# A hybrid diffusion layer: the output projection of the second token block as one seven-product pass

## The chip, the cores and the metric

The kernel runs on one core of one Trainium2 chip. The metric is device time in microseconds (us), the median of three runs. The profile is of one more execution, taken by the hardware profiler. Engines: PE (TensorE), with PEld for its weight loads, DVE (VectorE), ACT (ScalarE), POOL (GpSimd), and SP, whose queue issues every DMA of this kernel.

## The reference

One layer of a diffusion backbone over 2048 latent tokens of width 1024, with 256 context tokens before them. All in fp32:

```
hl  = rms(x) * norm1 * (1 + sc1) + sh1
z, xbc, dt, u, v = split(hl @ w_in)
ssd = rms_per_group((scan(conv(xbc), dt) + skip) * silu(z)) * ssd_norm   # 1024 wide, forward and backward scan
gm  = gelu(u) * (W_s @ rms(gelu(v)) + b_s)                               # 1024 wide, per 128 tokens
x   = x + g1 * (concat(gm, ssd) @ w_out)                                 # w_out 2048 x 1024
hl2 = rms(x) * norm2 * (1 + sc2) + sh2
x   = x + g2 * ((silu(hl2 @ w_gate) * (hl2 @ w_up)) @ w2)                # hidden width 2816
out = rms(x) * final_norm
```

`sc1`, `sh1`, `g1` and the like come from the conditioning vector. The context tokens only give the scans their start states.

## The kernel before

Everything is stored with channels on the 128 partitions and tokens along the row. The 2048 tokens are two blocks of 1024 (block 1 is computed first, since the backward scan starts at its end), each block two groups `j` of 512 tokens. A matmul is 128x128 stationary by 128x512 moving. Each fp32 operand is split into a high and a low part of a reduced type (a ScalarE cast and a VectorE subtract), and each product is three matmuls: high by high, high by low, low by high.

The stages follow each other so. (1) Block 1: `xbc`, then one interleaved run (L937) with the main sequence `proj_v`, `proj_u`, `proj_z` and, beside it, context scan, backward scan, row statistics and `ada_rest`, which loads 16 MB of modulation weights. (2) Block 0: `xbc`. (3) A second interleaved run (L943): the main sequence `proj_z`, `proj_v`, `proj_u`, then `out_half(1, 0)`, `out_half(0, 0)`, `out_half(0, 1)`; beside it the rest of the backward scan and the whole forward scan `ssd_y`. (4) `out_half(1, 1)` alone. (5) `prep_hl(0)`, then `ffn1(0)`, `ffn2(0)` with `prep_hl(1)` beside it, `ffn1(1)`, `ffn2(1)`.

`run` (L871) alternates generators: after each `yield` of the main sequence it advances the other one by a ratio, 1.4 side steps in (1) and `SIDE` = 2.74 in (3). A main step is one output tile, 24 matmuls; `ssd_y` and the backward scan of block 0 have 256 side steps. This program order is a priority: a planner then gives each engine a fixed order of instructions by its own cost estimates and by the buffers that come free, and on the chip each engine and SP take theirs in order.

The output projection works by halves of the inner width: half 0 takes `gm` (kept in `gmscr`), half 1 the scan's output (kept in `sscr` by `y_store`, L781). `out_half` has for each block and half eight output tiles `m` by two groups `j`, each eight inner tiles by three matmuls; it adds to the residual `x2scr` in DRAM. Its moving operands are loaded and split by `load_mix` (L819) into 16 tiles `actt`, its weights are loaded by `unit` (L201) three ahead and split. The sum of squares for the second norm is taken on the way, and its inverse root is stored in `r2scr`.

The feed-forward uses seven products in place of eight (a Strassen scheme) for each 2x2 arrangement of tiles. `prep_hl` (L980) reads `x2scr` and `r2scr`, scales and shifts, forms the four sums that the scheme needs and splits them into 28 tiles `hl`. `ffn1` forms the weight sums on GpSimd as it goes; `ffn2` (L1129) runs product by product: for each product `p` of seven and each inner step `i` it loads two 128x512 tiles (activations from `ascr`, weights from `wscr` or `wall`) into one buffer `w4`, splits it into two buffers `hl4`, and issues four banks by three matmuls. Loads go four steps ahead, splits two. Results accumulate in two sets of four PSUM banks, and after the last step of a product its banks are added to the residual tiles.

The feed-forward's pools (`hlp`, 112 KB per partition; `t2p`, `w4p`, `hlw`, 92 KB) are opened after `mix` and `pjs`, the pools of all that came before, are closed:

```
    for _ in out_half(1, 1, s1):
        pass
    mix.close()
    pjs.close()
    ...
    hl, g = prep_hl(0)
    for _ in g:
        pass
    ffn1(0, hl)
```

## Time and profile before

| | |
|---|---|
| median of 3 runs | 3014.0 us (3011.1 to 3016.5) |
| the profiled execution | 3005.2 us, span 3003.4 us |
| TensorE busy | 94% of the span, 12474 matmuls |
| VectorE, ScalarE, GpSimd busy | 67%, 43%, 21% |
| DMA | 515 MB, mean 172 GB/s |
| granted TensorE clock, mean | 0.967 |

The page cuts the span into 40 slices of 75 us; a digit is the busy share in tenths, PEclk the granted clock in tenths of full speed. By time, (1) reaches to about 590, (2) to 765, (3) to 1551, (4) to 1639, and the feed-forward fills the rest.

### The profile page before, as it was taken

Reading aid. Unit: us, or ns where it says so; the run is one execution under the profiler, and the core shown is the slowest. Engines: PE = TensorE matmul, PEld = TensorE weight load, DVE = VectorE, ACT = ScalarE, POOL = GpSimd, SP = SyncE. Lnnn points to the kernel's source line nnn. Section 1 sums busy time; section 2 is a strip of 40 time slices with the busy share of each in tenths; the row PEclk is TensorE's granted clock in tenths of the full one; section 3 lists DMA queues with packets and bytes.
Section 4 is the critical chain, followed back from the end, with each engine's and each line's share of the span. In section 5 each row is a group of like instructions: output and inputs, shape, how many; then the busy total and the mean of one; then the engine's idle time right before and its main releaser. Section 6 shows DMA issues by size and latency. Waiting matters only on the chain. (4 is left out here: it accounts for less than half of the span.)

```text
span 3003.4 us, 37067 instructions
## 1 busy us (share of the span) xinstructions
PE 2818.3 (94%) x12474; PEld 2252.2 (75%) x12474; DVE 2017.5 (67%) x3412; ACT 1295.1 (43%) x2387; POOL 642.9 (21%) x550
## 2 busy tenths in 40 slices
PE   7999999999999888999898699999999899999997
PEld 3787778878677766777676488888778788888885
DVE  6777966885788878877653755556776644445555
ACT  4444343344355555445442433333554333333443
POOL 3100000110131222223100444445120322221000
PEclk8999999999999999999999699999999999999998
DMA  5322567732755668778644344444766433334764
GB/s 221 97 90 83 190 220 232 257 118 88 240 152 155 209 197 253 239 237 250 197 150 122 106 162 158 158 158 168 257 227 201 150 101 100 102 102 134 235 194 155
DMA packets 289771, 515.45 MB, mean 172 GB/s; under 512 B 28198, under 2 KB 88998, under 8 KB 289580
## 3 DMA queue, kind: packets, MB, share of 16 engines
q1 hardware_dynamic: 289580, 513.08, 53.4%
q8 instruction: 98, 1.61, 0.2%
q14 instruction: 93, 0.76, 0.1%
HBM read 375.60 MB, written 137.38 MB: 171 GB/s over the span
## 5 line engine op out<-in xcount | busy, mean ns | idle before, releaser
L970 DVE TENSOR_TENSOR hl<-w,hl 128x1024 fp32r<-128x1024 f32 x286 | 373.8, 1313 | 313.5 <-ACT hl L969 130.3
L969 ACT CAST hl<-w 128x1024 fp32r<-128x1024 f32 x286 | 299.2, 1051 | 435.9 <-PE mmp L1053 126.7
L228 PE MATMUL mmp<-actt,whi 128*128 128x512 f32 x1120 | 455.5, 407 | 6.2 <-DVE tma L575 6.2
L229 PE MATMUL mmp<-actt,whi 128*128 128x512 f32 x1120 | 445.5, 398 | 0.0
L230 PE MATMUL mmp<-actt,wlo 128*128 128x512 f32 x1120 | 444.2, 397 | 0.0
L1052 PE MATMUL mmp<-hl,hl 128*128 128x512 f32 x704 | 277.7, 394 | 37.1 <-ACT hl L969 32.4
L1053 PE MATMUL mmp<-hl,hl 128*128 128x512 f32 x704 | 276.9, 393 | 2.4 <-DVE hl L970 2.4
L1054 PE MATMUL mmp<-hl,hl 128*128 128x512 f32 x704 | 276.7, 393 | 0.0
L228 PEld LDWEIGHTS mmp<-actt,whi 128*128 128x128 f32 x1120 | 214.7, 192 | 55.4 <-DVE tma L575 7.5
L229 PEld LDWEIGHTS mmp<-actt,whi 128*128 128x128 f32 x1120 | 214.5, 191 | 48.1 <-issue 5.3
L230 PEld LDWEIGHTS mmp<-actt,wlo 128*128 128x128 f32 x1120 | 214.5, 192 | 47.6 <-issue 1.7
L228 PE MATMUL mmp<-whi,actt 128*128 128x512 f32 x512 | 212.1, 414 | 0.0
L1052 PE MATMUL smp<-hl,hl 128*128 128x512 f32 x528 | 209.1, 396 | 1.7 <-ACT hl L969 1.6
L1053 PE MATMUL smp<-hl,hl 128*128 128x512 f32 x528 | 207.5, 393 | 0.0
L1054 PE MATMUL smp<-hl,hl 128*128 128x512 f32 x528 | 207.3, 393 | 0.1
L230 PE MATMUL mmp<-whi,actt 128*128 128x512 f32 x512 | 206.9, 404 | 0.0
L229 PE MATMUL mmp<-wlo,actt 128*128 128x512 f32 x512 | 206.3, 403 | 0.0
L1052 PEld LDWEIGHTS mmp<-hl,hl 128*128 128x128 f32 x704 | 133.7, 190 | 67.6 <-ACT hl L969 34.8
L976 DVE TENSOR_TENSOR t<-smp,t 128x512 f32<-128x512 f32 x88 | 60.5, 687 | 180.5 <-PE smp L1054 105.9
L450 DVE SCALAR_TENSOR_TENSOR tma<-xin,cw,tma 128x512 f32<-128x512 f32 x192 | 144.3, 751 | 21.8 <-ACT tma L448 16.2
L1053 PEld LDWEIGHTS mmp<-hl,hl 128*128 128x128 f32 x704 | 133.9, 190 | 31.2 <-DVE hl L970 3.5
L731 POOL TENSOR_TENSOR tma<-tma 128x512 f32<-128x512 f32 x64 | 88.9, 1389 | 319.8 <-ACT tma L730 223.0
(256 smaller groups left out, 5816.5 us busy)
## 6 DMA issues: line engine op xcount, KB each, us to landing
w<-in_wall_dram SPq DMA_DIRECT2D x110, 512.0 KB, 4.0
ws<-in_wall_dram SPq DMA_DIRECT2D x104, 512.0 KB, 4.2
ascr<-t SPq DMA_DIRECT2D x154, 256.0 KB, 4.1
w<-ascr SPq DMA_DIRECT2D x154, 256.0 KB, 2.7
tma<-fscr SPq DMA_DIRECT2D x128, 256.0 KB, 5.5
w<-wscr SPq DMA_DIRECT2D x88, 256.0 KB, 3.5
w<-in_wall_dram SPq DMA_DIRECT2D x66, 256.0 KB, 4.0
rec<-tma SPq DMA_DIRECT2D x64, 256.0 KB, 2.6
```

Source lines behind the costliest of these rows:

```text
L228: PE.matmul(ps, lhsT=lh, rhs=rh, start=(i == 0), stop=False)
L229: PE.matmul(ps, lhsT=lh, rhs=rl, start=False, stop=False)
L230: PE.matmul(ps, lhsT=ll, rhs=rh, start=False, stop=(i == n - 1))
L450: V.scalar_tensor_tensor(out=acc[:, :n], in0=raw[:, j:j + n], scalar=cw[:, ch, j:j + 1], in1=acc[:, :n], op0=ALU.mult, op1=ALU.add)
L731: G.tensor_tensor(out=A, in0=A, in1=fb, op=ALU.mult)
L969: S.copy(hi, x)
L970: eng.tensor_tensor(out=lo, in0=x, in1=hi.bitcast(F32), op=ALU.subtract)
L976: eng.tensor_tensor(out=o, in0=a, in1=b, op=ALU.add)
L1052: PE.matmul(ps, lhsT=hi[:, ms_], rhs=t[:, 0, :], start=first and k == 0, stop=False, skip_group_check=not first)
L1053: PE.matmul(ps, lhsT=hi[:, ms_], rhs=t[:, 1, :], start=False, stop=False, skip_group_check=not first)
L1054: PE.matmul(ps, lhsT=lo[:, ms_], rhs=t[:, 0, :], start=False, stop=k == 3, skip_group_check=not first)
```

## The change

The output projection of block 0 stays as it was. That of block 1 becomes one pass of seven products over both halves, by the routine of `ffn2`, which is made general (`product_major`) and gives a `yield` after each step. The pass, `out_pm(1)`, has eight inner steps in place of the feed-forward's eleven; four take `gm`, four the scan's output.

Its operands are built earlier. `proj_u(1)` forms the sums of `gm` tiles (two subtracts on GpSimd, two on VectorE for each pair of heads) and stores seven tiles in `ogm` instead of four. `y_store` stores the chunks 8 to 11 unchanged in `osd`; for each of the chunks 12 to 15 it reads two of those back, does four subtracts on VectorE and stores five tiles. `wo_sums`, at the end of the side sequence of (1), loads the projection's weights (given once more as `wok`), scales them on ScalarE, forms four sums on GpSimd for each of eight groups and stores seven tiles per group in `owt`; the ratio there becomes 1.6.

The pass is the end of the main sequence of (3): after `out_half(0, 1)` the pool `pjs` is closed and the streaming buffers are opened in its place, on the right side of the memory. The side sequence goes on after `ssd_y` with `prep_hl(0)`, six side steps for each of its four parts, once `mix` is closed. Two product steps count as one main step, and the pass does not go beyond its eighth step before `ssd_y` is done. `SIDE` becomes 3.1.

```diff
-SIDE = 2.74
+SIDE = 3.1
...
+    wp = pjs.enter_context(tc.tile_pool(name="wp", bufs=NWP, side="right"))
+    ws = pjs.enter_context(tc.tile_pool(name="ws", bufs=2, side="right"))
+    ap_ = pjs.enter_context(tc.tile_pool(name="act", bufs=16, side="right"))
+    xi = pjs.enter_context(tc.tile_pool(name="xin", bufs=NX, side="right"))
...
+    sp = mix.enter_context(tc.tile_pool(name="sml", bufs=8))
...
+    ogm = [tc.dram_tile([7, P, TB], F32, name=f"ogm{i}") for i in range(4)]
+    osd = [tc.dram_tile([4, P, TB], F32, name=f"osd{i}") for i in range(7)]
+    owt = [tc.dram_tile([7, P, TB], F32, name=f"owt{i}") for i in range(8)]
...
-    order += (list(range(U_O, U_O + 8)) * 2 + list(range(U_O + 8, U_O + 16)) * 2)
+    order += list(range(U_O, U_O + 16))
...
+            bs = {}
...
-                    t = gelu2(ps, tmp)
+                    t = gelu2(ps, xin if blk else tmp)
                     V.tensor_tensor(out=t[:, :TB], in0=t[:, :TB], in1=m[:, :TB], op=ALU.mult)
-                    DMA.dma_start(gmscr[h0 + i][:, ts_], t[:, :TB])
+                    if blk == 0:
+                        DMA.dma_start(gmscr[h0 + i][:, ts_], t[:, :TB])
+                    else:
+                        bs[i, j] = t[:, :TB]
+                        if len(bs) == 4:
+                            b11, b12, b21, b22 = bs[0, 0], bs[0, 1], bs[1, 0], bs[1, 1]
+                            t1, tt, t4 = tmp()[:, :TB], tmp()[:, :TB], tmp()[:, :TB]
+                            sub(t1, b12, b11, G)
+                            sub(tt, b22, t1, V)
+                            sub(b12, b22, b12, G)
+                            sub(t4, b21, tt, V)
+                            for q, x in ((1, b11), (2, b21), (6, tt), (5, t1), (7, b12), (3, b22), (4, t4)):
+                                DMA.dma_start(ogm[h0 // 2][AQ[q]], x)
...
     def y_store(ys, c):
+        bs = []
         for g in range(2):
             ps = smp()
             for i in range(4):
                 PE.transpose(out=ps[:, i * P:(i + 1) * P], in_=ys[g][:, i * P:(i + 1) * P], identity=ident)
             t = tma()[:, :TB]
             S.copy(t, ps)
-            DMA.dma_start(sscr[c // 4][g * TB:(g + 1) * TB, (c % 4) * P:(c % 4 + 1) * P].rearrange("(i p) t -> p i t", p=P),
-                          t.rearrange("p (i t) -> p i t", t=P))
+            if c < 8:
+                DMA.dma_start(sscr[c // 4][g * TB:(g + 1) * TB, (c % 4) * P:(c % 4 + 1) * P].rearrange("(i p) t -> p i t", p=P),
+                              t.rearrange("p (i t) -> p i t", t=P))
+            bs.append(t)
             yield
+        if c < 8:
+            return
+
+        def osl(q):
+            return osd[AQ[q]][:, :, (c % 4) * P:(c % 4 + 1) * P].rearrange("i p t -> p i t")
+
+        def v4(t):
+            return t.rearrange("p (i t) -> p i t", t=P)
+
+        if c < 12:
+            DMA.dma_start(osl(1), v4(bs[0]))
+            DMA.dma_start(osl(2), v4(bs[1]))
+            return
+        b12, b22 = bs
+        b11, b21, tt = tma()[:, :TB], tma()[:, :TB], tma()[:, :TB]
+        DMA.dma_start(v4(b11), osl(1))
+        DMA.dma_start(v4(b21), osl(2))
+        sub(b11, b12, b11, V)
+        sub(tt, b22, b11, V)
+        sub(b12, b22, b12, V)
+        sub(b21, b21, tt, V)
+        for q, x in ((6, tt), (5, b11), (7, b12), (3, b22), (4, b21)):
+            DMA.dma_start(osl(q), v4(x))
...
+    def wo_sums():
+        for i in range(8):
+            k1, k2 = (2 * i, 2 * i + 1) if i < 4 else (4 + i, 8 + i)
+            q = []
+            for k in (k1, k2):
+                for h in range(2):
+                    t = tma()[:, :TB]
+                    DMA.dma_start(t, wok[k][:, h * TB:(h + 1) * TB])
+                    S.activation(t, t, AF.Copy, scale=0.5 if i < 4 else vec[:, V_SN + k - 8:V_SN + k - 7])
+                    q.append(t)
+            a0, a1, b0, b1 = q
+            s1, s2, s4 = tma()[:, :TB], tma()[:, :TB], tma()[:, :TB]
+            add(s1, a1, b1, G)
+            sub(s2, s1, a0, G)
+            sub(s4, b0, s2, G)
+            sub(a1, a0, a1, G)
+            for p, x in ((1, a0), (2, b0), (6, s2), (5, s1), (7, a1), (3, s4), (4, b1)):
+                DMA.dma_start(owt[i][AQ[p]], x)
...
-        (chain(ssd_ctx(rp, hp), ssd_bwd(rp, hp, range(15, 7, -1)), stats_x(0, tma), stats_x(1, tma), ada_rest(tma)), 1.4))
+        (chain(ssd_ctx(rp, hp), ssd_bwd(rp, hp, range(15, 7, -1)), stats_x(0, tma), stats_x(1, tma), ada_rest(tma), wo_sums()), 1.6))
...
-    m1, m0, s0, s1, h2 = [], [], [], [], []
-    run((chain(proj_z(0, hs), proj_v(0, hs), early(proj_u(0, hs), 16, 6, lambda: [load_mix(2, 0), load_mix(3, 0)], m1),
-               early(out_half(1, 0, m1), 16, 4, lambda: [load_mix(0, 0), load_mix(1, 0)], m0),
-               early(out_half(0, 0, m0), 16, 4, lambda: [load_mix(0, 1), load_mix(1, 1)], s0),
-               early(out_half(0, 1, s0), 16, 2, lambda: [load_mix(2, 1), load_mix(3, 1)], s1)), 1),
-        (chain(ssd_bwd(rp, hp, range(7, -1, -1)), ssd_y(rp)), SIDE))
-
-
-    for _ in out_half(1, 1, s1):
-        pass
-    mix.close()
-    pjs.close()
-    hlp = ctx.enter_context(tc.tile_pool(name="hlp", bufs=1, reuse_waits="tile"))
-    t2p = ctx.enter_context(tc.tile_pool(name="t2p", bufs=NT2, reuse_waits="tile"))
-    w4p = ctx.enter_context(tc.tile_pool(name="w4p", bufs=NW4, reuse_waits="tile"))
-    hlw = ctx.enter_context(tc.tile_pool(name="hlw", bufs=NHL, reuse_waits="tile"))
+
+    fp = {}
+
+    def open_stream():
+        pjs.close()
+        for n, b in (("w4", NW4), ("hl4", NHL), ("t2", NT2)):
+            fp[n] = ctx.enter_context(tc.tile_pool(name=n + "p", bufs=b, side="right", reuse_waits="tile"))
+
+    def open_hl():
+        mix.close()
+        fp["hl"] = ctx.enter_context(tc.tile_pool(name="hlp", bufs=1, reuse_waits="tile"))
...
-    def ffn2(blk, side):
-        NK = NJ // 2
-        steps = [(p, i) for p in STR_P for i in range(NK)]
-        raw, rdy = {}, {}
-        bank = {}
-        x2 = {}
+    def product_major(nk, aload, wload, upd):
+
+        steps = [(p, i) for p in STR_P for i in range(nk)]
+        raw, rdy, bank = {}, {}, {}
 
         def load(n):
             p, i = steps[n]
             w = raw[n] = w4()
-            DMA.dma_start(w[:, A0], ascr[blk][i][AQ[p]])
-            if p in WQ:
-                src_ = wscr[i][WQ[p]]
-            else:
-                hh, c = {1: (2 * i, A0), 2: (2 * i + 1, A0), 4: (2 * i + 1, A1)}[p]
-                src_ = wall[U_F + 3 * hh + 2][:, c]
-            DMA.dma_start(w[:, A1], src_)
+            DMA.dma_start(w[:, A0], aload(p, i))
+            DMA.dma_start(w[:, A1], wload(p, i))
...
+            if i == nk - 1:
+                upd(p, bank[p])
+            yield
+
+    UPD = {1: (0, 0), 2: (0, 0), 6: (1, 0), 3: (1, 0), 5: (1, 4), 7: (1, 4), 4: (0, 4)}
+    DONE = {2: (0, 0), 7: (1, 4), 3: (1, 0), 4: (0, 4)}
+
+    def out_pm(blk):
+        x2, acc = {}, [None, None]
+
+        def upd(p, banks):
+            j, mo = UPD[p]
+            ts_ = slice((blk * 2 + j) * TB, (blk * 2 + j + 1) * TB)
+            for m in range(mo, mo + 4):
+                if (j, m) not in x2:
+                    x2[j, m] = t2()
+                    DMA.dma_start(x2[j, m], xT[m * P:(m + 1) * P, ts_])
+                x = x2[j, m]
+                V.scalar_tensor_tensor(out=x, in0=banks[m - mo], scalar=m_sb[:, 16 + m, 0:1], in1=x, op0=ALU.mult, op1=ALU.add)
+                if p in DONE:
+                    DMA.dma_start(x2scr[m][:, ts_], x)
+                    acc[j] = sq_acc(acc[j], x, t2)
+            if p in (3, 4):
+                rstd_store(acc[j], r2scr[blk * 2 + j], t2)
+
+        return product_major(8, lambda p, i: ogm[i][AQ[p]] if i < 4 else osd[AQ[p]][i - 4], lambda p, i: owt[i][AQ[p]], upd)
...
+        for _ in product_major(NJ // 2, lambda p, i: ascr[blk][i][AQ[p]], wload, upd):
...
-    hl, g = prep_hl(0)
-    for _ in g:
-        pass
-    ffn1(0, hl)
+    m0, s0, box = [], [], []
+
+    def main():
+        yield from proj_z(0, hs)
+        yield from proj_v(0, hs)
+        yield from early(proj_u(0, hs), 16, 2, lambda: [load_mix(0, 0)], m0)
+        m0.append(load_mix(1, 0))
+        yield from early(out_half(0, 0, m0), 16, 2, lambda: [load_mix(0, 1), load_mix(1, 1)], s0)
+        yield from out_half(0, 1, s0)
+        open_stream()
+        for i, _ in enumerate(out_pm(1)):
+            if i == 7:
+                while not box:
+                    yield
+            if i % 2:
+                yield
+
+    def side():
+        yield from ssd_bwd(rp, hp, range(7, -1, -1))
+        yield from ssd_y(rp)
+        open_hl()
+        hl, g = prep_hl(0)
+        box.append(hl)
+        for _ in g:
+            for _ in range(6):
+                yield
+
+    run((main(), 1), (side(), SIDE))
+    ffn1(0, box[0])
```

## Rows read from the trace of the kernel before

**Rows 1.** The page: busy time of TensorE, and its granted clock by slice.

```profile
PE 2818.3 (94%) x12474; PEld 2252.2 (75%) x12474; DVE 2017.5 (67%) x3412; ACT 1295.1 (43%) x2387; POOL 642.9 (21%) x550
...
PEclk8999999999999999999999699999999999999998
```

**Rows 2.** Busy us (instructions) per engine in a stretch, clock, DMA share, GB/s.

```profile
1639.00:1800.00 161.00, 120.25 (x467) 93.40 (x468) 105.28 (x117) 70.77 (x103) 74.24 (x44) 0.83 0.42 138
1725.00:2025.00 300.00, 300.00 (x1325) 248.51 (x1324) 174.74 (x174) 102.08 (x143) 146.85 (x96) 1.00 0.49 159
```

**Rows 3.** Timeline of TensorE after 1639: start, us, in brackets the idle time before.

```profile
1661.68 0.79 PE L1052 MATMUL mmp<-hl,hl 128*128 128x512 f32 x1 [19.74 <-ACT hl L969]
```

**Rows 4.** Groups of instructions from 1639 to 1706: busy us, mean ns, idle before.

```profile
L970 DVE TENSOR_TENSOR hl<-t,hl 128x512 fp32r<-128x512 f32 x29 | 25.7, 909 | 9.0 <-ACT hl L969 8.7
L973 POOL TENSOR_TENSOR t<-t,t 128x512 f32<-128x512 f32 x8 | 20.3, 2536 | 151.6 <-ACT hl L969 142.5 <-DVE hl L970 5.4 <-DMA t<-x2scr 3.6
L969 ACT CAST hl<-t 128x512 fp32r<-128x512 f32 x29 | 16.8, 614 | 24.0 <-POOL t L973 23.9
```

**Rows 5.** Busy times by stretch around the seams of the feed-forward.

```profile
2115.00:2130.00 15.00, 15.00 (x68) 12.40 (x67) 9.93 (x14) 7.47 (x12) 0.98 (x1) 1.00 0.95 324
2130.00:2145.00 15.00, 12.05 (x46) 9.46 (x45) 12.46 (x12) 8.60 (x10) 2.48 (x2) 0.89 0.68 222
2160.00:2235.00 75.00, 69.65 (x290) 56.29 (x290) 59.73 (x65) 44.25 (x57) 18.59 (x8) 0.95 0.70 230
2325.00:2370.00 45.00, 36.79 (x143) 28.62 (x142) 30.44 (x37) 18.01 (x22) 16.03 (x11) 0.89 0.53 184
```

**Rows 6.** DMA issues: transfer, count, KB each, median us from issue to landing.

```profile
tma<-in_wad_dram SPq DMA_DIRECT2D x64, 256.0 KB, 4.9
...
gmscr<-tma SPq DMA_DIRECT2D x32, 256.0 KB, 2.7
```

**Rows 7.** Two lines of the kernel: duration in ns, least, median and most.

```profile
L970 DVE TENSOR_TENSOR hl<-w,hl x286: 1209/1225/2315, 1661.7 to 2973.2; 128x1024 fp32r<-128x1024 f32 x143
L970 DVE TENSOR_TENSOR hl<-t,hl x100: 676/682/1787, 1649.1 to 2752.3; 128x512 fp32r<-128x512 f32 x100
...
L997 DVE SCALAR_TENSOR_TENSOR t<-t,a,t x32: 736/745/1780, 1645.3 to 2212.8; 128x512 f32<-128x512 f32 x32
```

**Rows 8.** Groups of instructions on VectorE from 780 to 1640.

```profile
L215 DVE TENSOR_TENSOR wlo<-ws,whi 128x1024 fp32r<-128x1024 f32 x50 | 66.0, 1321 | 13.4 <-ACT whi L214 13.3
L848 DVE SCALAR_TENSOR_TENSOR tma<-mmp,m_sb,tma 128x512 f32<-128x512 f32 x64 | 47.7, 746 | 56.2 <-DMA tma<-x2scr 41.5 <-PE mmp L230 7.1 <-DMA tma<-fscr 3.9
```

**Rows 9.** Busy times by stretch in the second run, and their sum.

```profile
790.00:865.00 75.00, 72.63 (x322) 56.91 (x321) 56.47 (x124) 42.72 (x110) 24.30 (x20) 0.95 0.70 210
865.00:1290.00 425.00, 379.95 (x1729) 297.92 (x1729) 362.99 (x890) 234.85 (x638) 110.35 (x90) 0.95 0.67 204
1290.00:1540.00 250.00, 229.76 (x1023) 180.07 (x1021) 179.03 (x387) 118.74 (x274) 58.48 (x47) 0.95 0.70 215
sum 750.00, PE 682.33 PEld 534.90 DVE 598.49 ACT 396.31 POOL 193.13; mean PE 227.44 PEld 178.30 DVE 199.50 ACT 132.10 POOL 64.38
```

**Rows 10.** Waits from 780 to 1640: who for whom, us in total, times, longest.

```profile
DVE tma L848 <- DMA tma<-x2scr: 41.5, 19, 6.2
```

**Rows 11.** Busy times by stretch in the first run and the stage after it.

```profile
290.00:390.00 100.00, 98.34 (x439) 73.10 (x438) 92.69 (x278) 37.16 (x134) 0.00 (x0) 1.00 0.56 182
390.00:540.00 150.00, 145.26 (x643) 118.11 (x642) 97.75 (x188) 55.58 (x89) 1.63 (x1) 1.00 0.72 236
540.00:690.00 150.00, 146.68 (x677) 121.99 (x676) 127.49 (x205) 66.20 (x100) 23.09 (x46) 0.99 0.53 170
```

**Rows 12.** Timeline from 1668: GpSimd and VectorE.

```profile
1669.51 1.58 POOL L973 TENSOR_TENSOR t<-t,t 128x512 f32<-128x512 f32 x1 [0.69 <-DVE hl L970]
1669.89 1.75 DVE L997 SCALAR_TENSOR_TENSOR t<-t,a,t 128x512 f32<-128x512 f32 x1
```

**Rows 13.** Timeline of SP's queue from 1640: start, us, transfer, count.

```profile
1640.28 1.97 SPq L996 DMA_DIRECT2D t<-x2scr  x4
1647.89 0.23 SPq L265 DMA_DIRECT2D r2scr<-tma  x1
```

More of the change, by code (lines that the diff above doesn't have):

```diff
@@ L82 @@
 def kernel(ctx: ExitStack, tc: tile.TileContext, xT, ctxp, cc, crow, wad1, wad2, vecs, rows,
-                             gmb, wall, wdt, gmw, csts, outT, dbg=None):
+                             gmb, wall, wok, wdt, gmw, csts, outT, dbg=None):
     nc = tc.nc
@@ L242, in newton, with sub, add @@
         return y
+    def sub(o, a, b, eng):
+        eng.tensor_tensor(out=o, in0=a, in1=b, op=ALU.subtract)
+    def add(o, a, b, eng):
+        eng.tensor_tensor(out=o, in0=a, in1=b, op=ALU.add)
     def rstd_of(ps, n, mk):
@@ L970, in split @@
         eng.tensor_tensor(out=lo, in0=x, in1=hi.bitcast(F32), op=ALU.subtract)
-    def sub(o, a, b, eng):
-        eng.tensor_tensor(out=o, in0=a, in1=b, op=ALU.subtract)
-    def add(o, a, b, eng):
-        eng.tensor_tensor(out=o, in0=a, in1=b, op=ALU.add)
     A0, A1 = slice(0, TB), slice(TB, D)
     def prep_hl(blk):
-        hl = {(p, k): hlp.tile([P, 2, TB], F32R, name=f"hl{p}_{k}", tag=f"hl{p}_{k}") for p in STR_P for k in range(4)}
+        hl = {(p, k): fp["hl"].tile([P, 2, TB], F32R, name=f"hl{p}_{k}", tag=f"hl{p}_{k}") for p in STR_P for k in range(4)}
         rb = []
@@ L1151, in prep @@
             rdy[n] = (hi, lo)
-        def upd(p, m):
-            j, mo = {1: (0, 0), 2: (0, 0), 6: (1, 0), 3: (1, 0), 5: (1, 4), 7: (1, 4), 4: (0, 4)}[p]
-            if (j, mo + m) not in x2:
-                x = x2[j, mo + m] = t2()
-                DMA.dma_start(x, x2scr[mo + m][:, (blk * 2 + j) * TB:(blk * 2 + j + 1) * TB])
-            x = x2[j, mo + m]
-            V.scalar_tensor_tensor(out=x, in0=bank[p][m], scalar=m_sb[:, 40 + mo + m, 0:1], in1=x, op0=ALU.mult, op1=ALU.add)
-        acc = [None, None]
         LD, PP = 4, 2
@@ L1174, in ffn2 @@
             hi, lo = rdy.pop(n)
-            fst, lst, cont = i == 0 and p in (1, 2, 5), i == NK - 1, p not in (1, 2, 5)
+            fst, lst, cont = i == 0 and p in (1, 2, 5), i == nk - 1, p not in (1, 2, 5)
             for m in range(4):
@@ L1180, in ffn2 @@
                 PE.matmul(bank[p][m], lhsT=lo[:, ms_], rhs=hi[:, A0], start=False, stop=lst, skip_group_check=cont)
-            if i == NK - 1:
-                for m in range(4):
-                    upd(p, m)
-                    j, mm = {2: (0, m), 7: (1, 4 + m), 3: (1, m), 4: (0, 4 + m)}.get(p, (None, None))
-                    if j is not None:
-                        acc[j] = sq_acc(acc[j], x2[j, mm], t2, (G, V)[j] if p != 4 else V)
-                if p == 3:
-                    final(blk, 1, x2, acc[1])
-                if p == 4:
-                    final(blk, 0, x2, acc[0])
+            if i == nk - 1:
+                upd(p, bank[p])
@@ new lines, in ffn2, with wload, upd @@
+    def ffn2(blk, side):
+        x2, acc = {}, [None, None]
+        def wload(p, i):
+            if p in WQ:
+                return wscr[i][WQ[p]]
+            hh, c = {1: (2 * i, A0), 2: (2 * i + 1, A0), 4: (2 * i + 1, A1)}[p]
+            return wall[U_F + 3 * hh + 2][:, c]
+        def upd(p, banks):
+            j, mo = UPD[p]
+            for m in range(mo, mo + 4):
+                if (j, m) not in x2:
+                    x2[j, m] = t2()
+                    DMA.dma_start(x2[j, m], x2scr[m][:, (blk * 2 + j) * TB:(blk * 2 + j + 1) * TB])
+                x = x2[j, m]
+                V.scalar_tensor_tensor(out=x, in0=banks[m - mo], scalar=m_sb[:, 40 + m, 0:1], in1=x, op0=ALU.mult, op1=ALU.add)
+                if p in DONE:
+                    acc[j] = sq_acc(acc[j], x, t2, (G, V)[j] if p != 4 else V)
+            if p in (3, 4):
+                final(blk, j, x2, acc[j])
+        for _ in product_major(NJ // 2, lambda p, i: ascr[blk][i][AQ[p]], wload, upd):
@@ L1265, in _layout @@
         "wad1": g["w_ada"][0][:, :2048].reshape(4, 2, P, 4, TB).transpose(3, 0, 2, 1, 4).reshape(16, P, D),
-        "wad2": g["w_ada"][0][:, 2048:].T.reshape(32, P, D), "vecs": vecs, "rows": rows, "gmb": g["gm_bs"][0].reshape(1, -1), "wall": wall,
+        "wad2": g["w_ada"][0][:, 2048:].T.reshape(32, P, D), "vecs": vecs, "rows": rows, "gmb": g["gm_bs"][0].reshape(1, -1), "wall": wall, "wok": wo.reshape(16, P, D),
         "wdt": w_in[:, 4608:].reshape(KT, P, 32).transpose(1, 0, 2).reshape(P, KT * 32),
```

12 lines of the change are left out of this document (4 added, 8 removed).

## The prediction

> **What bounds the kernel now.** I read the page first: TensorE is busy 94% of the span, and its clock row stands at 8 to 9 everywhere but for one 6 just past the middle [rows 1]. So TensorE is the resource, a removed matmul is worth its full issue time where TensorE is saturated, and the slice with the 6 is a hole. The busy times by stretch give the rate and the hole [rows 2]: in the feed-forward, 1325 matmuls in 300 us, 0.2264 us each; from the end of the output projection at 1639 to 1800, 467 in 161 us, worth 467 x 0.2264 = 105.7 us. **The hole costs 55.3 us.** The timeline of TensorE shows how it begins: 19.7 us of waiting for a ScalarE cast of the feed-forward's operands, then a matmul of 0.79 us, at the lower of the clock's two levels [rows 3]. The groups of instructions in the hole say what runs there: VectorE and ScalarE build the 28 tiles `hl` (`prep_hl(0)`), with GpSimd in between, and TensorE has nothing else [rows 4].
>
> **The change part by part.** The sum is made against the profiled execution's own 3005.2 us (span 3003.4), 8.8 us below the median of 3014.0.
>
> *Matmuls.* Block 1's two halves issue 2 x 8 x 2 x 24 = 768 matmuls; the pass issues 7 products x 8 steps x 12 = 672. 96 fewer x 0.2264 = **-21.7 us**.
>
> *The hole.* `prep_hl(0)` now runs beside the pass: **-55.3 us**. Late next is the feed-forward's first weight preparation, behind the pass's last step. The same seam stands in the trace where block 0's second feed-forward part ends and block 1's first begins: 143 matmuls in 45 us, where 199 would fit, 12.6 us lost [rows 5]. The new seam has the same loads, buffers and row statistics: **+12.6 us**.
>
> *Start of the pass.* Its buffers lie over those of the half before, so its third and later tiles wait for that half's last matmuls. A streaming pass starts in the trace at 2130: 46 matmuls in 15 us, where 66 fit: **+4.6 us** [rows 5]. From below it is nothing (the first two steps are loaded ahead), from above a landing of 4.9 us and a split of 1.2 [rows 6, 7].
>
> *`prep_hl(0)` beside the pass.* It yields six times per quarter and gets 3.1 side steps per two product steps, so it falls into some 16 product steps, 16 x 12 x 0.2264 = 43.5 us. VectorE then has 16 splits at 1.225 = 19.6, `prep_hl`'s 36 subtracts at 0.682 and 16 scalings at 0.745 = 36.5, and eight evictions at 0.746 and four sums of squares at 0.682 = 8.7: 64.8 us [rows 7, 8]. Of the excess of 21.3, two steps prepared ahead hide 5.4: **+16 us**. Bounds: the same job beside a streaming pass, at ten steps a quarter, left 290 matmuls in 75 us, 9.3 us lost [rows 5]; and 30 with VectorE slowed as in the hole, where the subtract of 0.682 takes 0.909 on average [rows 4].
>
> *The scan's stretch.* The scan has the same 256 side steps, but at 3.1 per main step in place of 2.74 they meet 82.6 main steps in place of 93.4: some 11 projection steps (59.7 us of matmuls) leave the stretch and are paid in the pass. What changes is the density. From 790 to 1540 VectorE is busy 598.5 of 750 us (79.8%), TensorE 682.3 (91.0%); in the middle part VectorE is at 85.4% and TensorE at 89.4%, in the two others 72.5% and 93.0%, so 0.28 points of TensorE go with each point of VectorE [rows 9]. VectorE's new load: less 11 evictions with half a split each (15.5), less 16 operand builds priced like evictions (11.9), plus 16 subtracts in `y_store` (10.9): 582 us [rows 7, 8]. TensorE's remaining 622.6 us take 684 at today's share; VectorE is then at 85.1%, TensorE loses 1.5 points: **+11 us**. Bounds: 0, and 18 if the middle part gets denser by the same slope. `y_store` of the last four chunks also adds a wait: four subtracts on VectorE behind two loads issued just before. Such a load-then-VectorE wait took 41.5 us over 19 times [rows 10], 2.2 each, so 9 us of VectorE; the projection's evictions stand behind it, and TensorE has four banks of 5.4 us to go on with. The chunks' five stores (two before) are first needed by the third product, 16 steps or 43 us into the pass; that covers them.
>
> *Block 1's stretch.* `wo_sums` issues 32 loads, 32 scalings on ScalarE, 32 sums on GpSimd and 56 stores, 23 MB, in the last five main steps, on SP ahead of the next stage's weight loads; `proj_u(1)` adds 8 subtracts on VectorE, 8 on GpSimd and 12 stores. TensorE is at 98% there beside a VectorE at 93% in the first part and 85% in the last; the DMA engines carry 236 GB/s in the second part and 170 in the third [rows 11], where the densest slice of the trace has 324 [rows 5]. The 23 MB need 150 us of the third part's spare 154 GB/s, and nothing waits for them for 700 us. TensorE idles 8.1 us from 390 to 690; I let that grow by three quarters, **+6 us**. Bounds: 0, and 19 by this mechanism: a GpSimd subtract starts at 1669.5, and the VectorE instruction that starts beside it takes 1.75 us in place of 0.745 [rows 7, 12]. That is 1.0 us of VectorE for each of the 40 new GpSimd instructions if all collide, 41 us, of which VectorE's 22.5 idle us from 540 to 690 cover the rest but 19. I stay near the lower end, since TensorE kept 98% beside the 93% VectorE. A rule of the Trainium skill speaks against the change at this place: "SBUF — State Buffer", section "SBUF: two separate sides", has GpSimd and a VectorE instruction with two SBUF inputs exclude each other for a whole instruction. The trace agrees for the pair above; if it held for all 40, the sum would end 13 us higher, at 3000.
>
> Sum: -21.7 - 55.3 + 12.6 + 4.6 + 16 + 11 + 6 = **-26.8 us**, 2978.4 for a profiled execution, and with the 8.8 us to the median **2987 us**.
>
> **Rivals.**
> *The weight sums block the queue (slower).* If one round of `wo_sums` must finish before the next one's loads go out, a round takes 4.9 landing + 0.6 scaling + 4 x 1.58 on GpSimd + 2.7 for the stores = 14.5 us, eight take 116 [rows 4, 6, 12]. Five main steps (27 us) and four banks (22 us) cover 49; TensorE waits 67 in place of 6, and the change costs 34 us: 3048. It turns to a loss from 33 us of waiting, about ten us a round. For it: SP is in order, and from 1642 to 1647.9 it stood before one small store whose data was late [rows 13]. Against it: loads that belong behind such a store went out ahead of it at 1640.3 [rows 13], so the order isn't the program's, and the 14 buffers hold two rounds of seven.
>
> *Half cover.* `prep_hl(0)` crowds out the splits of the pass, whose lead is two steps, and the clock falls after each wait as in the hole; 39 us are lost in place of 16: -4 us, 3010. For it: 64.8 us of VectorE in 43.5. Against: 9.3 us lost at the slower pace.
>
> *All hidden.* 9.3 for `prep_hl`, nothing in the two scan stretches: -50.5 us, 2963. For it: TensorE at 98% beside VectorE at 93%. Against: the slope of 0.28.
>
> *It doesn't do what it says.* The scan ends so late that the third product waits, and the pass stands idle where the hole was. The scan would have to slip by 43 us, where the slope gives 11; the price beyond that is one us for each, some 3010 at 23 us more.
>
> **How the numbers follow.** Forecast 0.50, own range 2972 to 3003 (its terms off by some half of their bounds); all hidden 0.18; half cover 0.15; weight sums 0.13; the last 0.04. 0.2%, 6 us, is about what a measurement of this kernel can tell from no change. Faster: the first two and a fifth of half cover, 0.71. Same: most of the other half covers and the last, 0.12. Slower: the sums and the rest, 0.17. The range of 2955 to 3030 takes in the all-hidden case and reaches towards 3048; it leaves out about 2 in 10.
>
> **What would show it.** Right: 672 matmuls on the pass's lines; no stretch of 50 us at half the matmul rate before the feed-forward, but a seam of some 12 us; VectorE above 90% in the pass's second third, with TensorE waiting there for splits; TensorE at 89 to 90% in the scan's stretch. Wrong: over 30 us of TensorE waits at the end of block 1's stretch and in the stage after it (weight sums), over 30 us inside the pass (half cover), or a wait for the pass's loads from `osd` before the third product.

## The result, and the profile after

The changed kernel takes 3145.9 us (median of 4 runs, 3141.0 to 3150.3) against 3012.8 beside it: a ratio of 1.045 (95% interval 1.0431 to 1.0469), 133 us slower where 27 us faster was forecast. Its profiled span is 3140.0 us, 136.6 above that of before. The page of the changed kernel, the lines that answer to [rows 1], and the slices of VectorE:

```profile
PE 2857.0 (91%) x12378; PEld 2255.2 (72%) x12378; DVE 2052.0 (65%) x3440; ACT 1338.4 (43%) x2427; POOL 689.8 (22%) x590
...
DVE  6777867518678978878588545555685644444555
...
PEclk9999999979899989999979999999999999999998
```

The 96 matmuls are gone and so is the 6 in the clock row. But in the ninth slice, at 628 to 706 us, where block 0's `xbc` runs, VectorE has a 1 and the clock a 7, and the clock has a second 7 at 1570 to 1648, around the start of the pass. The busy times by stretch around the first (columns as in [rows 2]):

```profile
600.00:625.00 25.00, 24.25 (x106) 19.39 (x105) 8.57 (x11) 11.33 (x19) 13.89 (x14) 1.00 0.55 197
625.00:650.00 25.00, 21.32 (x83) 17.13 (x82) 4.04 (x4) 7.96 (x14) 9.67 (x14) 0.86 0.74 245
650.00:675.00 25.00, 24.67 (x109) 20.08 (x107) 3.77 (x3) 5.76 (x8) 11.49 (x10) 1.00 0.70 238
675.00:700.00 25.00, 0.00 (x0) 0.00 (x0) 3.77 (x2) 7.49 (x10) 11.89 (x8) 0.53 0.65 234
700.00:725.00 25.00, 7.52 (x29) 6.08 (x30) 13.65 (x15) 9.29 (x13) 7.12 (x8) 0.58 0.63 220
```

VectorE works 4 of 25 us and TensorE goes on with its banks until, from 675, it stands still. What ended its wait, from the waits of 580 to 725 (who for whom, us in total, times, longest), and what SP issues meanwhile (start, us, line, transfer, count):

```profile
DVE wlo L218 <- ACT whi L217: 69.3, 7, 15.8
ACT tma L918 <- DMA tma<-in_wok_dram: 63.5, 10, 11.1
...
PE smp L471 <- DVE tma L463: 42.8, 1, 42.8
```

```profile
642.41 1.94 SPq L917 DMA_DIRECT2D tma<-in_wok_dram  x4
646.91 0.33 SPq L927 DMA_DIRECT2D owt<-tma  x1
647.28 0.43 SPq L214 DMA_DIRECT2D ws<-in_wall_dram  x1
648.44 7.56 SPq L927 DMA_DIRECT2D owt<-tma  x6
656.09 0.41 SPq L676 DMA_DIRECT2D zscr<-tma  x1
656.54 2.03 SPq L917 DMA_DIRECT2D tma<-in_wok_dram  x4
```

The second fence is a round of `wo_sums`: four loads, then the stores, over six of which SP spends 7.6 us, since they wait for scalings and sums, then the next loads 14.1 us after the last. Eight rounds run one by one from 591 to 715. ScalarE, in order too, stands at the scalings for their loads (63.5 us), its casts of the next weights behind them, and VectorE behind the casts (69.3). The convolutions (L459 to L463), for which TensorE waits its 42.8 us, are in VectorE's order behind these splits, and start only when the last round's is done:

```profile
709.55 1.40 DVE L218 TENSOR_TENSOR wlo<-ws,whi 128x1024 fp32r<-128x1024 f32 x1 [12.82 <-ACT whi L217]
710.87 4.99 DVE L459 SCALAR_TENSOR_TENSOR tma<-xin,cw,tma 128x512 f32<-128x512 f32 x4
```

The second slow place is the feed-forward's first part, all along it. The stretch of 300 us that answers to the 1325 matmuls in [rows 2]:

```profile
1860.00:2160.00 300.00, 300.00 (x1282) 241.18 (x1281) 158.25 (x165) 98.18 (x137) 139.14 (x92) 1.00 0.46 151
```

TensorE never waits and the clock is full, yet it issues 1282: 234.3 ns a matmul (start to start) in place of 226.7. The third is around the pass; the stretch of the pass, and from TensorE's timeline (start, us, in brackets the wait) the two waits ahead of it and the one behind it:

```profile
1595.00:1789.00 194.00, 171.36 (x712) 136.08 (x712) 151.17 (x184) 104.99 (x133) 27.82 (x15) 0.93 0.72 234
```

```profile
1579.57 2.04 PE L272 MATMUL smp<-tma,ones 128*128 128x512 f32 x2 [12.63 <-DVE sml L243]
1594.73 1.65 PE L1219 MATMUL mmp<-hl 128*128 128x512 f32 x3 [8.14 <-ACT hl L1032]
...
1805.75 2.08 PE L272 MATMUL smp<-t,ones 128*128 128x512 f32 x2 [13.16 <-DVE t L267]
```

672 of the 712 matmuls are the pass's; they are worth 152.3 us and take 194. From the last matmul ahead of the pass to its first, TensorE stands most of 28 us, the two waits above among them.

### The profile page after: what moved, and what is told of

The parts are those of the page before. It is cut to its first block, busy times and chain, and to the rows that moved or that the text cites. A ratio compares the mean times of both kernels' runs of the same rounds, so it can differ in the third digit from the quotient of the medians.

```text
span 3140.0 us, 37299 instructions
## 1 busy us (share of the span) xinstructions
PE 2857.0 (91%) x12378; PEld 2255.2 (72%) x12378; DVE 2052.0 (65%) x3440; ACT 1338.4 (43%) x2427; POOL 689.8 (22%) x590
## 5 line engine op out<-in xcount | busy, mean ns | idle before, releaser
L1033 DVE TENSOR_TENSOR hl<-w,hl 128x1024 fp32r<-128x1024 f32 x342 | 437.1, 1285 | 362.9 <-ACT hl L1032 146.5
L1032 ACT CAST hl<-w 128x1024 fp32r<-128x1024 f32 x342 | 357.4, 1051 | 492.6 <-PE mmp L1110 164.7
L231 PE MATMUL mmp<-actt,whi 128*128 128x512 f32 x864 | 355.0, 411 | 4.4 <-ACT xin L526 4.4
L233 PE MATMUL mmp<-actt,wlo 128*128 128x512 f32 x864 | 345.6, 400 | 0.0
L232 PE MATMUL mmp<-actt,whi 128*128 128x512 f32 x864 | 345.2, 400 | 0.0
L1109 PE MATMUL mmp<-hl,hl 128*128 128x512 f32 x704 | 280.1, 398 | 3.6 <-DVE t L1265 2.4
L1110 PE MATMUL mmp<-hl,hl 128*128 128x512 f32 x704 | 279.8, 398 | 0.0
L1111 PE MATMUL mmp<-hl,hl 128*128 128x512 f32 x704 | 279.7, 397 | 0.0
L1109 PE MATMUL smp<-hl,hl 128*128 128x512 f32 x528 | 211.6, 401 | 0.0
L1111 PE MATMUL smp<-hl,hl 128*128 128x512 f32 x528 | 210.1, 398 | 0.0
L1110 PE MATMUL smp<-hl,hl 128*128 128x512 f32 x528 | 210.1, 398 | 0.0
L1220 PE MATMUL mmp<-hl,hl 128*128 128x512 f32 x480 | 191.0, 398 | 8.9 <-DVE hl L1033 8.8
L231 PEld LDWEIGHTS mmp<-actt,whi 128*128 128x128 f32 x864 | 166.9, 193 | 44.4 <-issue 5.8
L1219 PE MATMUL mmp<-hl 128*128 128x512 f32 x480 | 187.3, 393 | 9.1 <-ACT hl L1032 9.1
L232 PEld LDWEIGHTS mmp<-actt,whi 128*128 128x128 f32 x864 | 166.6, 193 | 38.4 <-issue 5.1
L233 PEld LDWEIGHTS mmp<-actt,wlo 128*128 128x128 f32 x864 | 166.3, 193 | 35.5 <-issue 1.0
L1221 PE MATMUL mmp<-hl,hl 128*128 128x512 f32 x480 | 189.1, 394 | 0.0
L251 POOL TENSOR_TENSOR w<-w 128x512 f32<-128x512 f32 x44 | 60.3, 1371 | 574.5 <-DVE hl L1033 432.8
```

The costliest lines, as they stand in the source:

```text
L231: PE.matmul(ps, lhsT=lh, rhs=rh, start=(i == 0), stop=False)
L232: PE.matmul(ps, lhsT=lh, rhs=rl, start=False, stop=False)
L233: PE.matmul(ps, lhsT=ll, rhs=rh, start=False, stop=(i == n - 1))
L251: eng.tensor_tensor(out=o, in0=a, in1=b, op=ALU.add)
L1032: S.copy(hi, x)
L1033: eng.tensor_tensor(out=lo, in0=x, in1=hi.bitcast(F32), op=ALU.subtract)
```

## The experiments

"Profiled" is the span of a run's profiled execution, to be held against 3003.4 before and 3140.0 after. A stage's time runs from its first matmul to the next stage's; by this, (1) ends at 573 us and (2) at 730 in the kernel before, somewhat earlier than the times given above for them. Each group of runs had its own runs of the kernel before beside it (medians 3003 to 3015), so a ratio compares within a group, while profiled spans of different groups can differ by some 10 us with nothing changed.

**The weight sums left out** (e1), and the ratio of block 1's run back at 1.4 as well (e2).

```diff
-  ..., ada_rest(tma), wo_sums()), 1.6))
+  ..., ada_rest(tma)), 1.6))             # e2: 1.4
-  lambda p, i: owt[i][AQ[p]]
+  lambda p, i: wok[i + AQ[p]][:, A1]
```

> Leaves the weight sums (wo_sums) out; the pass reads raw weights in their place; ratio 1.6 kept. Theory A (the sums' rounds hold the ring of 14 tma buffers and SP's queue, VectorE starves, and block 0's stages are late): from the first projection of block 1 on, proj_z(1) back from 113 to 90-100 us, xbc(0) from 202 to 157, proj_z(0) from 166 to about 130; total 3146 less 95 to 110, 3036 to 3051. Theory B (the denser interleaving, 1.6 and 3.1, is the loss): proj_z(1) stays near 113, proj_z(0) near 160, total above 3090.

> As the first, with the ratio of the first run back at 1.4. If the ratio alone costs: proj_z(1) falls from what the first shows to 87 us and the total by the same 5 to 15 us. If only the sums cost: the same as the first within 6 us.

e1: ratio 1.0199 (1.0173 to 1.0225), profiled 3061.4, so 78.6 us less than with the sums. `xbc` of block 0 falls from 201.6 to 151.5 us and the stage after it, `proj_z`, from 166.0 to 137.4: that is where the rounds were paid. The total, 3066.2, stays above theory A's range, and block 1's `proj_z` stays at 112.8 (87.0 in the kernel before), as theory B had it. e2: 1.0174 (1.015 to 1.0198), profiled 3055.4. Block 1's `proj_z` falls to 96.2; on the total the ratio of 1.6 is worth 6 to 8 us, which the two intervals don't tell from nothing.

**SIDE back at 2.74** in the changed kernel.

> The changed kernel with SIDE back at 2.74, nothing else. Theory B: proj_z(0) and proj_u(0) come back (166 to about 130, 178 to about 150 us), the scan ends later beside the pass, total 3146 less 30 to 60. Theory A: proj_z(0) stays at 155 to 166 since its loss is the backlog of the sums, total within 20 us of 3146.

1.042 (1.0394 to 1.0445), profiled 3128.0. The stages from block 0's `proj_z` to the pass get 75 us shorter (28 of them in `proj_u`, 23 in the hole ahead of the pass), the pass 62 us longer (256.7), since it now waits for the scan. `proj_u` comes back as theory B had it; `proj_z` (154.2) and the total go by theory A. The scan takes 716 us in place of 730 although more main steps stand beside it: here they don't set its pace.

**The buffers' place alone**: the kernel before, with the feed-forward's pools opened as in the changed one.

```diff
-  hlp, t2p, w4p, hlw
+  w4p, hlw, t2p (side="right"), hlp
```

> The kernel before, with nothing changed but the place of the streaming buffers of the feed-forward (opened first and on the right side of the memory, as in the changed kernel). Theory C (the place of the buffers sets the matmul rate of ffn1, 234.3 ns a matmul after, 226.7 before): ffn1 at 234 ns, total 3013 plus 25 to 30. Rival: the rate follows from something else of the changed kernel (the clock, the DMAs): 226.7 ns and the same time within 6 us.

1.0105 (1.0085 to 1.0124): about 31 us for nothing but where the buffers lie. Its stretch 1725 to 2025 holds the same 1282 matmuls. The next four runs ask what about the place it is.

```diff
+    pad = ctx.enter_context(tc.tile_pool(name="pad", bufs=1))   # e5, e9: side="right", ahead of wp
+    gap = pad.tile([P, 8], F32, name="gap")        # 32 bytes; e18 [P, 32], e11 [P, 64], e9 [P, 344]
```

> The changed kernel with a gap of 32 bytes per partition ahead of the pools on the right side of the memory, so that the streaming buffers start at a multiple of 64 bytes (171968 in place of 172000) as in the kernel before (191104). Theory C1, the start of a buffer within 64 bytes sets the rate of the feed-forward's first part: 226.7 ns a matmul again there in place of 234.3, two times 1848 x 7.6 ns = 28 us less, 3118 us. Rival C2, it is the region of the memory (172000 to 208900 against 191100 to 228000) or the order of the pools: 234.3 ns stays, 3146 us.

> The kernel before with the same gap of 32 bytes ahead of t2p, w4p and hlw, which moves the streaming buffers from a multiple of 64 bytes to one of 32 and changes nothing else. C1: 234.3 ns a matmul in the feed-forward's first part in place of 226.7, 28 us slower, 3033 us, as with the pools moved to the right side. C2: 226.7 ns and 3004.5 us as before.

> The kernel before with a gap of 256 bytes ahead of t2p, w4p and hlw, so that the stationary tiles of the feed-forward's first part lie 256 bytes off the moving tiles within 512. C3 with a period of 256 bytes or less: 226.7 ns and 3004 to 3011 us as before. C3 with a period of 512 or more: 233 to 234 ns, 28 us slower, 3035. If neither: another rate, which would show that 226.7 is not the floor.

> The kernel before with a gap of 128 bytes ahead of t2p, w4p and hlw (32 bytes gave 233.3 ns a matmul in the feed-forward's first part, 256 gave 226.7). H1, the place counts with a period of 128 bytes: 226.7 ns, 3004 to 3012 us. H2, with 256: 233 ns, 3028 to 3037.

The same stretch of the kernel before with the 32-byte gap (e6), and that of the changed kernel with a gap of 1376 bytes (e9, below):

```profile
1725.00:2025.00 300.00, 300.00 (x1287) 241.51 (x1286) 166.00 (x169) 99.09 (x138) 143.81 (x94) 1.00 0.47 157
```

```profile
1860.00:2160.00 300.00, 300.00 (x1325) 248.49 (x1324) 171.58 (x173) 103.19 (x144) 143.15 (x95) 1.00 0.48 158
```

A multiple of 64 bytes was wrong (e5 has one: 233.3 ns, 3136.7 us), and so was the region. What orders all eight cases is the distance from the moving tiles `hl` (from byte 19072) to the stationary tiles, modulo 256. At 0 (before, e11, e9) the spacing is 226.7 ns; at 32 and 64 (e6, e5) 233.3; at 128 (e18) 232.4 in block 0's first part and 233.2 in block 1's; at 96 (after, and e4, which opens the same pools in the same order) 234.3. e11: ratio 0.9997 (0.9983 to 1.0011); e6: 1.0087 (1.0066 to 1.0107); e18: 1.0051 (1.0031 to 1.0071), some 15 us where its spacing gives 23. Why the distance counts, no run shows.

**Where the sums stand.** e7 puts a round after every eight side steps of block 1's run, e9 after every four (and has the gap of 1376 bytes).

```diff
-  chain(..., ada_rest(tma), wo_sums())
+  spread(chain(..., ada_rest(tma)), wo_sums(), 8)      # e9: 4
```

> The changed kernel with the eight rounds of weight sums spread over the whole side sequence of block 1, one after every eight side steps, at the same ratio of 1.6. Theory A1, it is the eight rounds in a row, 124 us long and in front of block 0's loads and convolutions, that starve the next stage: block 0's xbc comes back from 201.6 to 152 to 160 us and z0 from 166 to about 137, block 1's stages grow by 5 to 20 us, the total falls by 55 to 75 us, 3075 to 3090. Rival A2, each round costs its own 9 to 10 us wherever it stands (it holds seven of the 14 buffers and SP while its stores wait): the cost of 75 us only moves into block 1's stages, 3135 to 3150.

> The changed kernel with two edits that act in different stages. The eight rounds of weight sums come one after every four side steps from the start of block 1's run, so beside proj_v and proj_u, before the modulation weights are loaded; and the gap ahead of the right-hand pools is 1376 bytes, which puts the feed-forward's stationary tiles (170624) at the same place within 4096 bytes as its moving tiles (19072, and 191104 in the kernel before). Rounds: theory A3, a round is dear only where it shares the buffers, SP and the DMA engines with the modulation weights or with the convolutions (the first four rounds of the spread version cost some 2 us each): block 1's stages from v to z stay under 360 us, xbc0 at 152 to 160 and z0 at 130 to 140, the sums cost 15 to 35 us in all in place of 75. Rival A2, 9 us a round at any place: 400 us for v to z. Placement: theory C3, what counts is how the stationary and the moving tile lie to each other: 226.7 ns a matmul in the feed-forward's first part, 28 us less. Rival C2, the region: 234 ns stays. By A3 and C3 3055 us, by A2 and C2 3135.

e7: 1.0402 (1.0349 to 1.0456), profiled 3130.8. `xbc` and `proj_z` of block 0 are free (155.5 and 135.9), but block 1's `proj_z` goes from 112.8 to 159.0. e9: 1.0361 (1.0293 to 1.0429), profiled 3125.5, with the feed-forward's first parts 27.6 us shorter by the gap. Block 1's stages take 415.2 us, 77 more than without the sums (337.8, e1). So eight to ten us a round wherever it stands (e7's profiled span is 69 above e1's); A1 and A3 fall. The timelines of VectorE and GpSimd in e9 show a part of why:

```profile
436.32 0.16 DVE L246 SCALAR_TENSOR_TENSOR sml<-sml 128x4 f32<-128x4 f32 x1
436.52 1.20 DVE L247 SCALAR_TENSOR_TENSOR sml<-sml 128x4 f32<-128x4 f32 x1
437.64 0.68 DVE L587 SCALAR_TENSOR_TENSOR xin<-xin,mmp 128x512 f32<-128x512 f32 x1
...
439.11 1.19 DVE L246 SCALAR_TENSOR_TENSOR sml<-sml 128x4 f32<-128x4 f32 x1
440.33 1.19 DVE L247 SCALAR_TENSOR_TENSOR sml<-sml 128x4 f32<-128x4 f32 x1
```

```profile
436.40 1.29 POOL L254 TENSOR_TENSOR tma<-tma 128x512 f32<-128x512 f32 x1 [28.12 <-ACT tma L921]
437.78 3.72 POOL L251 TENSOR_TENSOR tma<-tma 128x512 f32<-128x512 f32 x3
```

While GpSimd works at its sums, VectorE instructions of 128x4 that take 0.16 us take 1.2. They are the chain of an inverse root, behind which a TensorE matmul (L638) waits 4.3 us. L587, between them, has one input in PSUM and takes its usual 0.68. The Trainium skill's rule that the forecast weighed ("SBUF — State Buffer", section "SBUF: two separate sides") speaks of two inputs in SBUF. The trace agrees.

**Two causes of a round's price.** From e9: the sums on VectorE (e13), the stores on GpSimd's queue (e14), both (e17).

```diff
-  add(s1, a1, b1, G) ... sub(a1, a0, a1, G)
+  add(s1, a1, b1, V) ... sub(a1, a0, a1, V)      # e13, e17
-  DMA.dma_start(owt[i][AQ[p]], x)
+  G.dma_start(owt[i][AQ[p]], x)                  # e14, e17
```

> The kernel with early rounds and the gap of 1376 bytes (e9: 3122 us, block 1's stages from v to z 415 us, 338 without the rounds), with the four sums of each round on VectorE in place of GpSimd. Theory E1, a round is dear because GpSimd's sums (5 us a round) hold up VectorE's short instructions and the chains behind them: v to z falls by 35 to 60 us, to 355 to 380, the total to 3062 to 3087. Rival E2, SP stands before the seven stores, or the seven buffers are held: 2.7 us of sums in place of 5 give 8 x 2.3 = 18 us at most, v to z 397 to 415. Rival E3, VectorE has no room: v to z above 415.

> The same kernel (e9) with the 56 stores of the rounds issued from GpSimd's queue in place of SP's, so that SP never stands before them; sums on GpSimd as before. E2 (SP): SP no longer spends 6.5 to 7.6 us a round there, v to z falls by 40 us or more, the total to 3080 or less. E1 (GpSimd holds up VectorE) or the buffers: v to z stays within 15 us of 415.

> The kernel with early rounds and the gap of 1376 bytes (e9: v to z 415 us, 3122 us), with both edits together: the four sums of a round on VectorE and its seven stores on GpSimd's queue. Alone they took 31 and 28 us off v to z. Theory G1, they are two costs: together 50 to 60 us, v to z 355 to 365, 3062 to 3075. Rival G2, they are one wait seen from two sides (SP stands because GpSimd is late): together 28 to 40 us, v to z 375 to 387, 3082 to 3095.

Block 1's stages take 384.1 us (e13), 387.2 (e14) and 373.9 (e17) against 415.2; ratios 1.0291 (1.0259 to 1.0323), 1.028 (1.0236 to 1.0325) and 1.0247 (1.0218 to 1.0277). Alone each saves about 30 us, between the ranges of E1 and E2 both times; together they save 41. That is just short of G2's range, and the total of 3088.7 lies within it: the two overlap for the larger part. 36 us stay, 25 of them in block 1's `proj_z`, where TensorE waits 43 us in place of e1's 19. Two waits make up 39 of the 43:

```profile
536.82 2.05 PE L275 MATMUL smp<-tma,ones 128*128 128x512 f32 x2 [18.38 <-DVE tma L270]
...
559.64 0.80 PE L234 MATMUL mmp<-whi,actt 128*128 128x512 f32 x1 [20.78 <-DVE tma L678]
```

The first is the row statistic of the same side sequence, which the rounds have pushed back: its matmul has a fixed place in TensorE's order and holds up the projections behind it. The same two waits stand in e9 (20.7 each). That a later place for the statistics would free them was not tried. Nor were two other suspects tested alone: ScalarE standing at the scalings for their loads, and the 14 buffers that the rounds share with their neighbours.

**The scan's pace.** e8 puts the forward scan ahead of nearly all of its cover in the kernel before; e12 is the kernel before with nothing but SIDE at 3.1.

```diff
+    run((proj_z(0, hs), 1), (ssd_bwd(rp, hp, range(7, -1, -1)), 1))
-    run((chain(proj_z(0, hs), proj_v(0, hs), ...), 1), (chain(ssd_bwd(...), ssd_y(rp)), SIDE))
+    run((chain(proj_v(0, hs), ...), 1), (ssd_y(rp), 8))      # e8
-SIDE = 2.74
+SIDE = 3.1                                                   # e12
```

> The kernel before with proj_z and the rest of the backward scan in a run of their own, one to one, and then the forward scan at eight side steps per main step, so that in program order the scan comes ahead of nearly all of its cover. Theory B1, the scan goes at the pace of its own chain of waits: a chunk takes 42 to 47 us as now (45.5), the projections fill in beside it, the total stays within 30 us of 3005. Rival B2, its pace is that of the main steps it is mixed with (the density of VectorE): a chunk falls below 38 us, and the later output projections run without the scan at 226.7 ns a matmul.

> The kernel before with SIDE at 3.1, so that 11 projection steps leave the scan's stretch and come behind it, without the pass. Theory of the prediction (B2): the scan's stretch gets shorter by the TensorE time that leaves it, 734 us to about 690, and the total grows by some 11 us, 3015. Theory B1, the scan has a pace of its own, of which a main step beside it takes only about 2 us (617 us with 33 steps beside it against 734 with 93): the scan's stretch stays at 710 to 735 us, and the 11 steps are paid behind it at 5.4 us each: 3035 to 3060.

```profile
855.00:1472.00 617.00, 413.79 (x1679) 303.52 (x1678) 484.98 (x1223) 318.82 (x893) 184.60 (x154) 0.80 0.56 161
```

In e8, above, the scan still takes 617 us with TensorE busy 67% of them and VectorE 79%: neither engine is full, so I take it that a good part of that time is its own chain of waits. (A chunk takes 37.9 us, at the edge of B2's range, and the total of 3191.8, ratio 1.0605, is far outside B1's: neither theory was right in its numbers.) In e12 the scan's stretch shrinks from 734 to 700 us for the 59.7 us of matmuls that leave it, and the stages from block 0's `proj_z` to the feed-forward grow from 931 to 957, by 26 us. The ratio, 1.0065 (1.0048 to 1.0082), gives 20 us (14 to 25): more than the prediction's 11, less than B1's total of 3035 to 3060, so neither theory is right here either.

**The operand building in `y_store`** (e15) and **the preparation behind the pass** (e16) and **paced slower beside it** (e10), all from e9.

```diff
-        b12, b22 = bs                    # e15
-        ... two loads, four sub, five stores
+        DMA.dma_start(osl(7), v4(bs[0]))
+        DMA.dma_start(osl(3), v4(bs[1]))
```
```diff
-        open_hl(); hl, g = prep_hl(0); box.append(hl) ... in side()
+        the same after run(...)          # e16
-            for _ in range(6):
+            for _ in range(14):          # e10
```

> The same kernel (e9) with y_store of the chunks 12 to 15 cut to two plain stores; the pass reads tiles that are there in place of the missing sums, so this part of the computation is left out (two loads, four subtracts and three stores per chunk). Theory F1, the operand building holds up the scan's chain: from the 12th to the 16th chunk the scan takes 145 to 155 us in place of 185, and the total falls by 25 to 40 us, to 3082 to 3097. Rival F2 (the prediction): 16 subtracts of 0.68, 11 us.

> The same kernel (e9) with prep_hl(0) behind the pass, as it stood behind the output projection before. The loss inside the pass is then that of the scan's tail and of the pass's own start. Theory D1, the preparation is what crowds the pass: the pass falls from 197 to 160 to 168 us, the hole of some 55 us comes back in place of the seam of 16, the total 3120 to 3135. Rival D2, it is the scan's tail: the pass stays at 180 us or more, the total 3145 to 3160.

> The kernel with the early rounds and the gap of 1376 bytes, and prep_hl(0) with 14 side steps per quarter in place of six, so that it covers some 36 product steps of the pass in place of 16. Theory D1, the pass loses its 42 us mostly because the preparation crowds VectorE in 43 us of it: the pass falls from 195 to 165 to 178 us. Rival D2, the loss is that of the scan's tail, which lies in the pass's first 40 us, and of loads: the pass stays above 187 us.

e15: 1.0332 (1.0301 to 1.0363), profiled 3102.8, 22.7 us less than e9; by the two ratios it is 9 us, within their intervals, so the places tell more than the total. The scan's stretch up to its twelfth chunk and from there to its last `y_store`, in the changed kernel, in e12 and in e15:

```profile
903.00:1450.00 547.00, 481.47 (x2133) 372.81 (x2132) 455.80 (x1115) 305.06 (x813) 156.59 (x126) 0.92 0.65 199
1450.00:1633.00 183.00, 144.59 (x611) 110.66 (x609) 127.55 (x259) 85.19 (x182) 37.47 (x29) 0.87 0.66 204
```

```profile
805.00:1360.00 555.00, 482.73 (x2159) 373.75 (x2158) 460.53 (x1117) 303.54 (x815) 155.72 (x126) 0.94 0.66 201
1360.00:1505.00 145.00, 126.63 (x569) 99.66 (x569) 107.48 (x233) 69.77 (x165) 35.96 (x28) 0.93 0.72 222
```

```profile
893.00:1446.00 553.00, 482.65 (x2145) 374.59 (x2143) 459.04 (x1116) 303.95 (x811) 160.38 (x126) 0.93 0.64 197
1446.00:1612.00 166.00, 141.04 (x597) 109.20 (x597) 117.27 (x245) 83.09 (x181) 36.22 (x29) 0.89 0.61 192
```

The first twelve chunks go nearly alike everywhere. In the last four the changed kernel is 38 us behind e12; leaving the building out returns 17 of them, and the hole ahead of the pass shrinks from 27.5 us in e9 to 13.0. F1's place is right, its size half. The rest of the 38 stays open. In the kernel before the two stretches take 564 and 170 us, so most of what e12 gains on it falls in the last four chunks, and there the changed kernel, at the same `SIDE`, takes even longer than the kernel before:

```profile
798.00:1362.00 564.00, 512.72 (x2329) 401.31 (x2328) 465.36 (x1121) 304.28 (x815) 155.63 (x125) 0.95 0.68 208
1362.00:1532.00 170.00, 153.70 (x673) 120.71 (x672) 125.32 (x262) 83.34 (x187) 36.23 (x31) 0.93 0.68 209
```

e16: 1.0461 (1.0428 to 1.0494), 15 us slower than e9 by the profiled spans and 30 by the ratios, so running the preparation beside the pass does pay. The total of 3143.8 lies between the two theories. Without the preparation the pass takes 171 us, just above D1's range and below D2's:

```profile
1592.00:1763.00 171.00, 163.81 (x712) 133.58 (x712) 111.21 (x132) 80.62 (x89) 7.69 (x5) 0.97 0.73 238
```

In e9 the pass takes 197 us, 45 more than its matmuls are worth; so some 26 of them are the preparation's and 19 belong to the scan's tail and the pass's own start. e10: 1.0347 (1.0282 to 1.0412); the pass stays at 195 us, so D1 falls on pace: spread out, the same VectorE work costs TensorE the same.

No form with the whole computation comes near the kernel before; the best is e17 with 3088.7 us.

## Why the prediction was wrong

The forecast was -26.8 us on profiled executions, the outcome +136.6: a miss of 163. Three steps of the sum carry it.

1. *"Block 1's stretch, +6"* (bounds 0 to 19) was the step that failed: 78.6 us for the weight sums, by e1. It was the rival of the sums that came true, at a chance of 0.13; its round of 14.5 us was right (14.4 on average from the second round on), its cover of 49 us was not. The rounds ran from 591 to 715 us, but block 1's stages ended at 601, and of the eight rounds' 115 us some 37 were covered. The main steps and banks do not cover rounds that hold up the next stage's own weight preparation (ScalarE) and loads (SP). My argument against it, that loads can go out ahead of waiting stores, fails in SP's rows: every round's loads stand behind the round before's stores. GpSimd's hold on VectorE, which I weighed at 13 us, stretches chains of small instructions too; the sums on VectorE save 31. Everything up to the end of block 0's `xbc` costs another 19 us without any sums (e1), 10 of them by the ratio of 1.6 (e2).

2. *A term that the sum lacked*: the place of the buffers. The forecast took from the change only that they lie on the right side, and gave that no price; the two first parts of the feed-forward have 3696 matmuls at 7.6 ns more, 28 us. e4 and e9 show it from both kernels.

3. *"The scan's stretch, +11."* The slope of TensorE's share over VectorE's took for granted that the scan goes as fast as the matmuls beside it. e8 and e12 show a pace of its own: matmuls taken out of its cover come back in time by about half (34 of 59.7 us in e12), which makes +26 by the stages and +20 by the ratio. `y_store`'s building adds 17 in the last four chunks (e15), where I had 11 us of VectorE work within that term.

The rest went by its sizes, but for the start of the pass. *Matmuls*, -21.7: 96 gone. *The hole*, -55.3: gone from its place; kept behind the pass it costs 15 to 30 us more than beside it (e16), and my terms for that move without the scan's tail give 55.3 - 12.6 - 16 = 26.7. *The seam*, +12.6: the wait at 1805.75 is 13.2, and the first part takes 435.8 in e9 where 1848 matmuls are worth 419, so 16.9. *The preparation*, +16 (9.3 to 30): some 26 (e16 against e9). *Start of the pass*, +4.6: 19 with the scan's tail, which the forecast kept out of the pass; and the hole of 28 us ahead of the pass (27.5 in e9, 13.0 in e15) had no term at all.

Of the signs that were named, the one for the weight sums came: 42.8 us of waiting in the stage after block 1's stretch. TensorE is busy 626 of 730 us in the scan's stretch, 86% in place of 89 to 90. VectorE's 91% stands in the first third of the pass, beside the scan's tail (59.5 of 65 us from 1595); the second third has 79%. No wait for `osd` shows.

The pieces were found one at a time and overlap, so they don't add up to the microsecond. By stages, e1 against before (profiled, 58.0 us in all): 19 up to the end of block 0's `xbc`; 10.5 from there to the end of the first feed-forward part, the 13.7 of the buffers' place taken off; 28 for that place in both blocks. With the 78.6 of the sums, 136.6.

## What to carry to other kernels

Work put "beside" a stage must be priced by the queues and the fixed orders it stands in, not by the spare share of the engines: a round of load, sum and store on an in-order queue can cost its latency to whoever is next in that queue. Before cover is taken away from a latency-bound stretch, measure its pace alone (e8) and with the ratio changed alone (e12). When buffers move, compare the matmul spacing in a stretch where TensorE never waits; here a distance between stationary and moving tiles that is a multiple of 256 bytes gave back 28 us.
